# Hybrid encoder: feed-forward chunk 5 by seven products too, and other engines for some low parts and sums

## The chip, the core and the metric

The kernel runs on one NeuronCore of a Trainium2 chip. TensorE (PE in the profile) multiplies, VectorE (DVE) and ScalarE (ACT) work element by element, GpSimd (POOL) and SyncE (SP) mostly issue DMA transfers. The metric is device time in microseconds of one execution; the median of the timed runs counts.

## What is computed

Two layers over x, 512 tokens by 1024 channels, in float32: a gated linear attention, then a grouped-query attention, each followed by a gated feed-forward part with a convolution of width 3 over the tokens. The change acts in the feed-forward part alone:

```python
def conv_ffn(h, w_up, w_conv, b_conv, w_down):
    u = h @ w_up                              # 1024 -> 2 x 2816
    u = lax.conv_general_dilated(u, w_conv[:, None, :], window_strides=(1,),
        padding=[(1, 1)], dimension_numbers=('NWC', 'WIO', 'NWC'),
        feature_group_count=u.shape[-1]) + b_conv
    val, gate = jnp.split(u, 2, axis=-1)
    return (jax.nn.silu(gate) * val) @ w_down # 2816 -> 1024

x = x + conv_ffn(rmsnorm(x, norm_ffn[i]), ffn_w_up[i], ffn_w_conv[i], ffn_b_conv[i], ffn_w_down[i])
```

## The kernel before

Everything is held transposed: channels on the 128 partitions, the 512 tokens along the free axis. A float32 factor is used as a high part, rounded to fp32r by ScalarE, and a low part, the rest. Each product takes three matmuls: high by high, high by low, low by high.

The 2816 hidden channels are 22 **chunks** m of 128, each with a val half and a gate half. A *plain* chunk (`plain_up`) takes 2 halves x 8 input tiles x 3 = 48 matmuls of 128x512. A chunk *by seven* (`seven_up`, for the chunks in `SEVEN`) treats val and gate, two input tiles and the two halves of the tokens as a product of 2x2 blocks, done with seven products in place of eight: 7 products x 4 pairs of input tiles x 3 = 84 matmuls of 128x256. Its seven products (`go(1 ...)` to `go(7 ...)`, in the order 1, 6, 7, 4, 5, 2, 3) all issue at line 1099 in `product`. Product 1 of chunk m+1 is begun half-way through chunk m. Between products ScalarE copies partial sums from one PSUM bank to another (L1158 in `twice`, L1122, L1131), and VectorE adds one (L1161 in `add_seven`).

A chunk by seven needs four **weight pieces**. Piece 0 is two quarters as loaded; piece 1 and piece 2 come from sums: VectorE adds two quarters (L312, 1024 wide) or two DMA transfers do it into a tile `sum` (chunks in `SUMS_DMA`); L314 then makes piece 1's. Piece 3, half as wide, comes after L303. The high part is ScalarE's L341 (L305 for piece 3), the low part VectorE's L342 (L306); that is `split`. The other way is `low_dma`: ScalarE writes the high part (L291) and its negative (L292), and a transfer issued by POOL (L330) adds the weights onto the negative, which gives the low part. `UP_DMA` names the plain chunks whose low parts go that way, `LOW_0` the chunks whose piece 0 does. Weights are loaded by SP into five `raw` buffers and worked on in the order of the queue `W.todo`, up to six pieces ahead of use.

The products by seven also need sums of input tiles. `prepare_input(p)` makes them for pair p with four VectorE operations in the tile `xr` and `low_dma` into the tiles `xt`; `INPUT_AT` says after which chunk. Chunks 0 to 2 use the normal input, later ones the tiles `nh` and `nl`.

After val and gate come the convolution (ScalarE L1146, VectorE L1147 and L1148), SiLU (L1150) and the product of the two (L1151). Two chunks of results are a pair, which `prepare` turns into the inputs `gu` of the down-projection by seven: sums (L1174 to L1176, L1186), then high parts by ScalarE (L1167) and low parts by VectorE (L1168), or all by `low_dma` for the pairs in `Q_DMA`. The down-projection runs in two parts by seven, after chunks 9 and 17, four output groups each, and the rest plain at the end. `end` adds each output chunk to the residual and, in the last layer, stores it.

Each engine works through its own instructions in order. The order in which they stand is made by a scheduler from the code; `tc.high_priority` and `tc.issue_after` move some of them.

Of the kernel before, what the change touches and what calls it, by code (L numbers as in the profile page):

```python
# [8 lines left out]
F32 = mybir.dt.float32  # L9
# [51 lines left out]


NQ, NPART = 4, 2
PLAIN = ([(c, k) for c in range(4) for k in range(16, 20)] + [(c, k) for c in range(4) for k in (20, 21)]
         + [(c, k) for c in range(4, 8) for k in range(16, 22)])
# [12 lines left out]
SUMS_DMA = (12, 13, 14, 15, 16)  # L78
SUMS_NEAR = 6
LOW_0 = (7, 8)  # L80
LOW_1 = ()
LOW_2 = ()
STRIP_0 = ()
# [2 lines left out]
NH = 4  # L86
NL = 4
LOADS_FFN = 3
WIDE_AT = 1
BACK_AT = 20  # L90
PAW = 6
UPAW = 3
# [10 lines left out]
def hybrid_encoder_kernel(  # L103
# [71 lines left out]

    prm = cp.tile([P, PC_N], F32, name="prm")

    fold = lambda t: t.rearrange("p (o n) -> p o n", n=S)

    class Weights:  # L180

# [55 lines left out]
        def load(self, key):  # L237
            src, i, h = key
            if i < 0:
                self.load_vg(src, -i, h)  # L240
            elif (id(src), i) in self.sums:
                if (id(src), i) not in self.strip:
                    t1, t3 = (pair("raw", NR, F32, "raw") for _ in range(2))
                    sync.dma_start(fold(t1), self.outer(src, i))
                    e = self.totals.pop((id(src), i), None)
                    if e is None:
                        sync.dma_start(fold(t3), self.outer(src, i, 1))
                    else:
                        sync.dma_start(t3[:, S:], src[i, :, 3 * S :])
# [23 lines left out]
            self.made[id(src), i, h] = (hi, lo)  # L273

        def outer(self, src, i, first=0):
            return src[i].rearrange("p (q n) -> p q n", q=4)[:, first : first + 3 : 2, :]

        def total(self, src, i):
            if any(src is a and i in SUMS_DMA for a in up) and (id(src), i) not in self.totals:
                self.totals[id(src), i] = e = big(F32, "sum")  # L280
                sync.dma_start(e, src[i, :, : 2 * S])
                self.pending.append((e, src[i, :, S : 3 * S]))

        def two(self):
            self.turn += self.wide
# [9 lines left out]
        def summed(self, src, i, h):  # L295


            tiles = self.strip[id(src), i]
            r, t3, e = tiles if h == 0 else [tiles[h % 3]] + tiles[1:]
            if h == 3:  # L300
                del self.strip[id(src), i]
                r = t3[:, S:]
                dve.tensor_tensor(r, r, t3[:, :S], ALU.add)  # L303
                hi, lo = (sp.tile([P, S], F32R, tag="sq", bufs=3, name=nm(n)) for n in ("wh4", "wl4"))
                act.activation(hi, r, AF.Copy)  # L305
                self.last = dve.tensor_tensor(lo, r, hi.bitcast(F32), ALU.subtract)  # L306
                return hi, lo
            if h == 1:
                with tc.issue_after(self.last.ins) if self.last else ExitStack():
                    if e is None:  # L310
                        tiles[2] = e = pair("raw", NR, F32, "sum")
                        dve.tensor_tensor(fold(e), t3[:, :S].rearrange("p (o n) -> p o n", o=1).to_broadcast([P, 2, S]),  # L312
                                          fold(tiles[0]), ALU.add)
                    dve.tensor_tensor(t3[:, :S], e[:, S:], tiles[0][:, :S], ALU.add)  # L314
                tiles[0] = None
            hi, lo = self.two()
# [14 lines left out]
            self.pending = []  # L331

        def split(self, hi, lo, r, pieces=1, first=False):
            n = 2 * S // pieces
            for q in range(pieces):
                sl = slice(q * n, (q + 1) * n)
                a = r[q] if isinstance(r, list) else r[:, sl]
                if first and q == 0:
                    dve.tensor_copy(hi[:, sl], a)
                else:  # L340
                    act.activation(hi[:, sl], a, AF.Copy)  # L341
                dve.tensor_tensor(lo[:, sl], a, hi[:, sl].bitcast(F32), ALU.subtract)  # L342
# [32 lines left out]
    def add_ffn(layer):  # L375
        first = 0
        for m, part in DOWN_AFTER.items():
            add_up(layer, range(first, m + 1))
            W.add(down_w[layer], range(part * NQ, (part + 1) * NQ), 4)
            at = len(W.todo) - 4 * NQ - 1  # L380
            W.todo[at : at + 2] = W.todo[at + 1], W.todo[at]
            first = m + 1
        add_up(layer, range(first, FC))
        W.add(down_w[layer], range(NPART * NQ, down_w[layer].shape[0]))

    W.add(w_first)
    W.add(w_kq, range(MORE // 2))
# [654 lines left out]
    def ffn(layer, norm, cw, nxt):  # L1042
# [47 lines left out]
        def product(pieces, src, strip, pairs, i, dst, start):  # L1090
            h, o = PLACE[i]
            if h not in pieces:
                pieces[h] = W.piece(src, strip, h, PAW if W.wide else PA)
            wh, wl = pieces[h]
            for j, p in enumerate(pairs):
                sl = slice(o + j * P, o + (j + 1) * P)
                mh, ml = p[i]
                for a, (w, m) in enumerate(((wh, mh), (wh, ml), (wl, mh))):
                    mm(dst, w[:, sl], m, start=start and j == 0 and a == 0, stop=j == len(pairs) - 1 and a == 2,  # L1099
                       skip_group_check=True)  # L1100
            W.flush()

        def begin_up(m):
            if m in SEVEN:
                begun.append(seven_up(m))
                next(begun[-1])

        def seven_up(m):

# [24 lines left out]
            begin_up(m + 1)  # L1134
            go(2, r1, False)
            go(3, r2, False)
            yield 0, both
# [68 lines left out]
                           7: part(1), 6: part(3), 4: part(2)})  # L1206


        PLACE = {1: (0, 0), 4: (0, S), 6: (1, 0), 2: (1, S), 7: (2, 0), 5: (2, S), 3: (3, 0)}

        def down_part(part, m):

# [57 lines left out]
        for m in range(FC):  # L1270
            if m == BACK_AT:
                W.loads, W.wide = LOADS, 0
                x_load()
            elif m == WIDE_AT:
                W.loads, W.wide, W.turn = LOADS_FFN, 1, 1
            held.append(act_up(m))
            for p in INPUT_AT.get(m, ()):
                prepare_input(p)
# [2 lines left out]
                    pass  # L1281
            if m % 2 == 0:
                continue
            if m < 2 * NQ * NPART:
# [6 lines left out]
            held = []  # L1291
        cur, open_ = None, {}
        for u, (c, k) in enumerate(PLAIN):
            if u % 8 == 0:
# [243 lines left out]
def _layout(inputs):  # L1538
# [69 lines left out]
    order += [(k, n) for n, k in PLAIN]  # L1608
    k, n = np.array(order).T
    dn = dn.transpose(0, 1, 3, 2, 4)[:, k, n]  # L1610
    a["w_down"] = con(dn.reshape(2, -1, 16, P, P).transpose(0, 1, 3, 2, 4).reshape(2, -1, P, 4 * S))
    return a

# [18 lines left out]
```

## Time and profile before

| | |
|---|---|
| median of 3 timed runs | 1088.42 us (1088.01 to 1088.79) |
| the profiled execution's own time | 1090.41 us |
| its span | 1088.7 us |
| chunks 3 to 8 of layer 0 in the trace | 252 to 326 us |
| the same chunks in layer 1 | 775 to 844 us |
| TensorE busy | 1077.5 us in 6744 matmuls |
| loads and stores | 172.41 MB by DMA, 158 GB/s in the mean |

A profile row of the timeline has its start, its duration, the engine, the line, the operation with its tiles (buffer numbers left out) and, in brackets, how long the engine had been idle before it and what it was waiting for. A row of a table by stretches has the busy time of each engine in that stretch. TensorE's matmuls overlap in the pipeline, so the distance between starts is the cost of one, not its duration.

### The profile page before, as it was taken

How to read it: one execution, taken by the hardware profiler on the slowest of the kernel's cores; microseconds unless marked ns; L12 is line 12 of the kernel's file. 1: busy time of each engine (PE TensorE's matmuls, PEld its weight loads, DVE VectorE, ACT ScalarE, POOL GpSimd, SP SyncE). 2: the span in 40 equal slices, each digit the busy share in tenths (PEclk: the TensorE clock that was granted, in tenths of full speed). 3: DMA queues.
4: the chain of work that ended last, by engine and by line, in shares of the span. 5: the costliest groups of instructions: out<-in, count | busy, mean ns of one | idle time of the engine just before them, and what ended most of it. 6: DMA issues, size and time to landing. Idle time of an engine off the chain costs nothing.

```text
span 1088.7 us, 17624 instructions
## 1 busy us (share of the span) xinstructions
PE 1077.5 (99%) x6744; PEld 970.9 (89%) x6744; DVE 887.3 (82%) x1329; ACT 728.5 (67%) x1146; POOL 146.3 (13%) x163
## 2 busy tenths in 40 slices
PE   9999999999999999999999999999999999999998
PEld 8888988888899999999988888788889999999996
DVE  7998967569698899978855578765989989997882
ACT  8679575478676777667664677646976667865760
POOL 0212112021100200010014343002210020001000
PEclk9999999999899999999999999999999999999999
DMA  8744546599534882265757475558964388226552
GB/s 301 185 126 107 123 144 208 156 207 213 114 124 99 216 215 101 78 161 131 258 134 182 104 221 146 167 173 186 215 135 150 97 215 222 96 78 159 133 175 78
DMA packets 69141, 172.41 MB, mean 158 GB/s; under 512 B 6848, under 2 KB 7360, under 8 KB 69056
## 3 DMA queue, kind: packets, MB, share of 16 engines
q1 hardware_dynamic: 47616, 115.28, 32.2%
q0 software_dynamic: 16544, 47.46, 24.1%
q10 hardware_dynamic: 4896, 8.55, 2.1%
q8 instruction: 53, 0.87, 0.3%
q14 instruction: 32, 0.26, 0.1%
HBM read 122.76 MB, written 14.68 MB: 126 GB/s over the span
## 4 chain that ended last, share of the span: by engine, by line
PE 91%; DVE 3%; DMA 2%; ACT 2%; issue 1%; POOL 0%; SPq 0%; DVEq 0%; ACTq 0%; POOLq 0%
PE r L1099 39%; PE op L560 8%; PE vg L677 7%; PE up L507 5%; PE up L508 5%; PE up L509 5%; PE dn L508 2%; PE dn L507 2%; PE dn L509 2%; DMA raw<-in_w_up_dram 1%; PE av L534 1%; PE A L507 1%; PE A L509 1%; PE B L509 1%; PE B L507 1%
## 5 line engine op out<-in xcount | busy, mean ns | idle before, releaser
L342 DVE TENSOR_TENSOR wl<-raw,wh 128x1024 fp32r<-128x1024 f32 x156 | 189.6, 1218 | 28.0 <-ACT wh L341 27.6
L341 ACT ACTIVATE wh<-raw 128x1024 fp32r<-128x1024 f32 x156 | 161.8, 1052 | 68.6 <-PE op L560 20.7
L1099 PE MATMUL r<-xt,wh 128*128 128x256 f32 x896 | 163.9, 284 | 2.6 <-ACT r L1122 2.6
L1099 PE MATMUL r<-gu,wh 128*128 128x256 f32 x896 | 161.0, 282 | 0.0
L1099 PEld LDWEIGHTS r<-xt,wh 128*128 128x128 f32 x896 | 140.8, 193 | 3.0 <-ACT r L1122 2.8
L1099 PEld LDWEIGHTS r<-gu,wh 128*128 128x128 f32 x896 | 139.4, 190 | 0.7
L1099 PE MATMUL r<-xt,wl 128*128 128x256 f32 x448 | 127.7, 285 | 0.0
L1099 PE MATMUL r<-gu,wl 128*128 128x256 f32 x448 | 126.6, 283 | 0.0
L1099 PE MATMUL r<-nh,wh 128*128 128x256 f32 x336 | 96.5, 287 | 0.2 <-ACT r L1131 0.2
L1099 PE MATMUL r<-nh,wl 128*128 128x256 f32 x336 | 95.0, 283 | 0.0
L1099 PE MATMUL r<-nl,wh 128*128 128x256 f32 x336 | 95.0, 283 | 0.0
L1099 PEld LDWEIGHTS r<-xt,wl 128*128 128x128 f32 x448 | 86.4, 193 | 0.0
L1099 PEld LDWEIGHTS r<-gu,wl 128*128 128x128 f32 x448 | 85.2, 190 | 0.0
L560 PE MATMUL op<-oT,wh 128*128 128x512 f32 x256 | 72.4, 393 | 0.0
L1099 PEld LDWEIGHTS r<-nh,wh 128*128 128x128 f32 x336 | 64.2, 191 | 2.7 <-ACT r L1131 2.2
L291 ACT ACTIVATE wh<-raw 128x1024 fp32r<-128x1024 f32 x36 | 38.0, 1056 | 42.2 <-PE up L508 13.3
L1099 PEld LDWEIGHTS r<-nl,wh 128*128 128x128 f32 x336 | 64.3, 191 | 0.1
L1099 PEld LDWEIGHTS r<-nh,wl 128*128 128x128 f32 x336 | 64.2, 191 | 0.0
L508 PE MATMUL up<-nl,wh 128*128 128x512 f32 x160 | 62.7, 392 | 0.0
L507 PE MATMUL up<-nh,wh 128*128 128x512 f32 x160 | 62.7, 392 | 0.0
L509 PE MATMUL up<-nh,wl 128*128 128x512 f32 x160 | 62.7, 392 | 0.0
L342 DVE TENSOR_TENSOR wl<-sum,wh 128x1024 fp32r<-128x1024 f32 x44 | 53.7, 1219 | 5.6 <-ACT wh L341 5.4
(300 smaller groups left out, 2752.3 us busy)
## 6 DMA issues: line engine op xcount, KB each, us to landing
raw<-in_w_up_dram SPq DMA_DIRECT2D x74, 512.0 KB, 4.9
raw<-in_w_down_dram SPq DMA_DIRECT2D x44, 512.0 KB, 4.1
wl<-raw POOLq DMA_DIRECT2D x20, 512.0 KB, 5.0
wl<-in_w_up_dram POOLq DMA_DIRECT2D x16, 512.0 KB, 8.1
ring<-p ACTq DMA_DIRECT2D x32, 256.0 KB, 2.5
sum<-in_w_up_dram SPq DMA_DIRECT2D x10, 512.0 KB, 6.9
sum<-in_w_up_dram POOLq DMA_DIRECT2D x10, 512.0 KB, 7.0
raw<-in_w_up_dram SPq DMA_DIRECT2D x18, 256.0 KB, 4.0
```

What stands on the lines that cost most here:

```text
L291: act.activation(hi, r, AF.Copy)
L341: act.activation(hi[:, sl], a, AF.Copy)
L342: dve.tensor_tensor(lo[:, sl], a, hi[:, sl].bitcast(F32), ALU.subtract)
L507: mm(ps, wh, mh, start=start, stop=False)
L508: mm(ps, wh, ml, start=False, stop=False)
L509: return mm(ps, wl, mh, start=False, stop=stop)
L534: mm(ps[j][:, :width], hl[k][i == 2][:, j * P : (j + 1) * P], (wl if i == 1 else wh)[:, sl], start=k == 0 and i == 0, stop=k == KC - 1 and ...
L560: mm(pss[ng][n], wt[:, sl], mv, start=k == late[0][0] and i == 0, stop=k == late[-1][-1] and i == 2)
L677: last = mm(ps[j], m[:, js], w[:, sl], start=i in (1, 7, 2) and p == 0 and a == 0, stop=i in (4, 2, 3) and p == 3 and a == 2, skip_group_c ...
L1099: mm(dst, w[:, sl], m, start=start and j == 0 and a == 0, stop=j == len(pairs) - 1 and a == 2, skip_group_check=True)
```

## The change

- `SEVEN` gets chunk 5. In `W.todo` the exchange of two entries where chunks by seven begin moves from chunk 6 to chunk 5.
- `INPUT_AT`: pair 3's input is prepared after chunk 3 with pair 2's, not after chunk 4.
- `UP_DMA`: of the plain chunks, 1, 2 and 4 get their low parts by DMA; before it was 1, 2 and 5.
- `LOW_0` is empty: piece 0 of chunks 7 and 8 is split by ScalarE and VectorE.
- `SUMS_DMA`: chunks 12 and 13 get their sums on VectorE, 14 to 16 by DMA as before.
- `Q_DMA`: pair 6's low parts are made by `low_dma`.
- `end`: the last output chunk is added in one operation and stored by one transfer; before it went in two halves over two queues.

All but the last hold for both layers. The remaining code of the diff (`TAIL`, `TAILED`, `tail_part`, `view`, `begin`) stands for a third way of the down-projection's rest; with `TAILED = ()` and `TAIL = 100` none of it runs. The layout of the weights in memory follows `SEVEN`. Its core:

```diff
-SEVEN = (6, 7, 8, 10, 11, 12, 13, 14, 15, 16, 18, 19, 20, 21)
+SEVEN = (5, 6, 7, 8, 10, 11, 12, 13, 14, 15, 16, 18, 19, 20, 21)
...
-INPUT_AT = {2: (0, 1), 3: (2,), 4: (3,)}
-Q_DMA = ()
-UP_DMA = (1, 2, 5)
-SUMS_DMA = (12, 13, 14, 15, 16)
+INPUT_AT = {2: (0, 1), 3: (2, 3)}
+Q_DMA = (6,)
+UP_DMA = (1, 2, 4)
+SUMS_DMA = (14, 15, 16)
 SUMS_NEAR = 6
-LOW_0 = (7, 8)
+LOW_0 = ()
...
-                if t == 0 and m not in DOWN_AFTER:
-                    begin_up(m + 1)
-                if t == 0 and m in DOWN_AFTER:
-                    down.append(down_part(DOWN_AFTER[m], m))
-                    next(down[-1])
+                if t == 0:
+                    begin(m)
...
-        def end(c, ps):
-            if nxt is not None or c < KC - 1:
+        def end(c, ps, last=False):
+            if nxt is not None or not last:
                 dve.tensor_tensor(x[c], x[c], ps, ALU.add)
```

The changed kernel is longer, so its lines have other numbers: L291 and L292 become L304 and L305, L303 and L306 L316 and L319, L312 and L314 L325 and L327, L330 L343, L341 and L342 L354 and L355, L1099 L1119, L1122 L1152, L1131 L1161, L1147 and L1148 L1177 and L1178, L1151 L1181, L1158 L1188.

ScalarE in layer 0's chunk 6, before. `r_2771` is the tile of chunk 6's partial sums, `raw_2679` the loaded quarters of chunk 8's piece 0:

```order
L341 ACTIVATE wh_2675<-raw_2631 128x1024
L1146 ACTIVATE y_2727<-up_2698,cw 128x512
L291 ACTIVATE wh_2774<-raw_2679 128x1024
L1122 ACTIVATE r_2771<-r_2696 128x256
L292 ACTIVATE wl_2775<-raw_2679 128x1024
L1158 ACTIVATE u_2791<-r_2773 128x512
L305 ACTIVATE wh_2755<-raw_2631 128x512
L1150 ACTIVATE y_2727<-y_2727 128x512
```

The same place in the changed kernel; here `r_2826` is chunk 6's, and `raw_2607` and `raw_2608` hold chunk 7's quarters:

```order
L1188 ACTIVATE r_2756<-r_2732 128x512
L318 ACTIVATE wh_2665<-raw_2559 128x512
L1176 ACTIVATE y_2728<-u_2700,cw 128x512
L1152 ACTIVATE r_2826<-r_2756 128x256
L1176 ACTIVATE y_2786<-r_2623,cw 128x512
L1188 ACTIVATE u_2845<-r_2828 128x512
L354 ACTIVATE wh_2770<-sum_2733 128x1024
L354 ACTIVATE wh_2736<-raw_2608 128x1024
```

The copy of chunk 6's partial sums (L1122, now L1152) stood right behind the high part of chunk 8's piece 0 (L291); now it stands between convolution starts, and the high parts that follow belong to chunk 7.

VectorE at chunk 8's pieces in layer 0, before; `raw_2679` and `raw_2680` are its quarters, `wl_2828` is piece 1's low part, `wl_2860` piece 2's:

```order
L312 TENSOR_TENSOR sum_2824<-raw_2680,raw_2679 128x1024
L1147 SCALAR_TENSOR_TENSOR y_2879<-r_2696,cw,y_2879 128x511
L314 TENSOR_TENSOR raw_2680<-sum_2824,raw_2679 128x512
L1148 SCALAR_TENSOR_TENSOR y_2879<-r_2696,cw,y_2879 128x511
L1151 TENSOR_TENSOR y_2879<-y_2879,y_2819 128x512
L342 TENSOR_TENSOR wl_2828<-raw_2680,wh_2827 128x1024
L342 TENSOR_TENSOR wl_2860<-sum_2824,wh_2859 128x1024
L303 TENSOR_TENSOR raw_2680<-raw_2680 128x512
```

And in the changed kernel, where `raw_2740` and `raw_2741` are chunk 8's quarters, `wl_2882` is piece 1's low part and `wl_2914` piece 2's:

```order
L325 TENSOR_TENSOR sum_2878<-raw_2741,raw_2740 128x1024
L1177 SCALAR_TENSOR_TENSOR y_2873<-u_2845,cw,y_2873 128x511
L327 TENSOR_TENSOR raw_2741<-sum_2878,raw_2740 128x512
L1178 SCALAR_TENSOR_TENSOR y_2873<-u_2845,cw,y_2873 128x511
L355 TENSOR_TENSOR wl_2914<-sum_2878,wh_2913 128x1024
L1177 SCALAR_TENSOR_TENSOR y_2933<-r_2756,cw,y_2933 128x511
L355 TENSOR_TENSOR wl_2882<-raw_2741,wh_2881 128x1024
L1178 SCALAR_TENSOR_TENSOR y_2933<-r_2756,cw,y_2933 128x511
L316 TENSOR_TENSOR raw_2741<-raw_2741 128x512
L1181 TENSOR_TENSOR y_2933<-y_2933,y_2873 128x512
```

Piece 2's low part now comes first, and both stand ahead of the addition L1181, which ends the convolution.

GpSimd's transfers from chunk 4 on in layer 0, before:

```order
L330 DMA wl_2481<-in_w_up_dram 128x1024
L330 DMA xt_2435<-xr_2212 128x1024
L330 DMA wl_2575<-in_w_up_dram 128x1024
L330 DMA xt_2443<-xr_2219 128x1024
L330 DMA xt_2524<-xr_2226 128x1024
L330 DMA xt_2618<-xr_2233 128x1024
L330 DMA wl_2669<-in_w_up_dram 128x2x512
L330 DMA wl_2775<-in_w_up_dram 128x2x512
```

And in the changed kernel:

```order
L343 DMA wl_2387<-in_w_up_dram 128x1024
L343 DMA xt_2434<-xr_2212 128x1024
L343 DMA wl_2478<-in_w_up_dram 128x1024
L343 DMA xt_2442<-xr_2219 128x1024
L343 DMA xt_2521<-xr_2226 128x1024
L343 DMA xt_2529<-xr_2233 128x1024
```

Chunk 4's low parts (`wl`, 128x1024) take the place of chunk 5's, pair 3's `xt` follows pair 2's at once, and the two transfers for chunks 7 and 8 (128x2x512) are gone.

More of the change, by code (lines that the diff above doesn't have):

```diff
@@ L88 @@
 LOADS_FFN = 3
+TAIL_SUMS = ()
 WIDE_AT = 1
+TURN = 1
 BACK_AT = 20
@@ L242, in load @@
                 if (id(src), i) not in self.strip:
-                    t1, t3 = (pair("raw", NR, F32, "raw") for _ in range(2))
+                    v, n = self.view(src, i)
+                    t1, t3 = (pair("raw", NR, F32, "raw")[:, : 2 * n] for _ in range(2))
                     sync.dma_start(fold(t1), self.outer(src, i))
@@ L275, in outer, with view @@
         def outer(self, src, i, first=0):
-            return src[i].rearrange("p (q n) -> p q n", q=4)[:, first : first + 3 : 2, :]
-        def total(self, src, i):
[L279 to L282, printed above, removed]
+            return self.view(src, i)[0].rearrange("p (q n) -> p q n", q=4)[:, first : first + 3 : 2, :]
+        def view(self, src, i):
+            if i < TAIL:
+                return src[i], S
+            row, part = divmod(i - TAIL, 2)
+            return src[NPART * NQ + row, :, part * 2 * S : (part + 1) * 2 * S], S // 2
+        def total(self, src, i):
+            if i in (SUMS_DMA if any(src is a for a in up) else TAIL_SUMS) and (id(src), i) not in self.totals:
+                v, n = self.view(src, i)
+                self.totals[id(src), i] = e = big(F32, "sum")[:, : 2 * n]
+                sync.dma_start(e, v[:, : 2 * n])
+                self.pending.append((e, v[:, n : 3 * n]))
         def two(self):
@@ L380, in add_ffn @@
             at = len(W.todo) - 4 * NQ - 1
-            W.todo[at : at + 2] = W.todo[at + 1], W.todo[at]
+            if m not in SEVEN:
+                W.todo[at : at + 2] = W.todo[at + 1], W.todo[at]
             first = m + 1
         add_up(layer, range(first, FC))
-        W.add(down_w[layer], range(NPART * NQ, down_w[layer].shape[0]))
+        if layer not in TAILED:
+            W.add(down_w[layer], range(NPART * NQ, down_w[layer].shape[0]))
+            return
+        w = down_w[layer]
+        for n in range(NQ):
+            W.sums.add((id(w), TAIL + n))
+            W.todo += [(w, TAIL + n, h) for h in range(4)]
+            if n % 2:
+                W.todo.append((w, NPART * NQ + NTAIL, n // 2))
     W.add(w_first)
@@ L1106, in begin_up, with begin @@
                 next(begun[-1])
+            if m == FC and layer in TAILED:
+                begun.append(tail_part())
+                next(begun[-1])
+        def begin(m):
+            if m in DOWN_AFTER:
+                down.append(down_part(DOWN_AFTER[m], m))
+                next(down[-1])
+            else:
+                begin_up(m + 1)
         def seven_up(m):
@@ L1254, in down_part, with tail_part, first, rest @@
                 W.pending.append((c, g))
-        def end(c, ps):
-            if nxt is not None or c < KC - 1:
+        def tail_part():
+            pairs = [quads.pop(NPART * NQ + i) for i in range(NTAIL)]
+            pieces = [{} for _ in range(NQ)]
+            go = lambda n, *a: product(pieces[n], w_dn, TAIL + n, pairs, *a)
+            st = {}
+            def first(n):
+                r = bank("pt", "r1")[:, :H]
+                go(n, 1, r, True)
+                st[n] = bank("acc", "r")
+                with tc.high_priority(200):
+                    twice(st[n], r)
+            def rest(n, cur):
+                for o, (c, ps) in enumerate(((2 * n + 1, third[n]), (2 * n, st[n]))):
+                    for k in range(2):
+                        at = ((n % 2) * 4 + 2 * o + k) * P
+                        sl = slice(at, at + P)
+                        mh, ml = plain[FC - 2 + k]
+                        for a, (w, mv) in enumerate(((cur[0], mh), (cur[0], ml), (cur[1], mh))):
+                            mm(ps, w[:, sl], mv, start=False, stop=k == 1 and a == 2, skip_group_check=True)
+                    end(c, ps, n == NQ - 1 and o == 1)
+            third = {}
+            first(0)
+            yield
+            for n in range(NQ):
+                r1, r2 = st[n][:, :H], st[n][:, H:]
+                go(n, 6, r2, False)
+                third[n] = r3 = bank("s", "r3")
+                with tc.high_priority(200):
+                    act.activation(r3[:, :H], r2, AF.Copy, scale=-1.0)
+                r4 = bank("pt", "r4")[:, :H]
+                go(n, 7, r4, True)
+                f = tmp("u", "f")
+                with tc.high_priority(200):
+                    twice(f, r4)
+                go(n, 4, r3[:, :H], False)
+                dve.tensor_tensor(x[2 * n + 1], x[2 * n + 1], f, ALU.add)
+                go(n, 5, r2, False)
+                with tc.high_priority(200):
+                    act.activation(r3[:, H:], r2, AF.Copy, scale=-1.0)
+                if n % 2 == 0:
+                    first(n + 1)
+                go(n, 2, r1, False)
+                go(n, 3, r2, False)
+                if n % 2:
+                    cur = W.half(w_dn, 2 * (NPART * NQ + NTAIL) + n // 2)
+                    rest(n - 1, cur)
+                    if n + 1 < NQ:
+                        first(n + 1)
+                    rest(n, cur)
@@ L1291, in ffn @@
             held = []
+        for steps in begun:
+            for _ in steps:
+                pass
+            return
         cur, open_ = None, {}
```

44 lines of the change are left out of this document (26 added, 18 removed).

## The prediction

> **What bounds the kernel now.** I read the page first, for the busy shares, then the chain that ended last, then TensorE's waits, and last the stretches of both layers' chunks 3 to 8, where the change acts.
>
> ```profile
> PE 1077.5 (99%) x6744; PEld 970.9 (89%) x6744; DVE 887.3 (82%) x1329; ACT 728.5 (67%) x1146; POOL 146.3 (13%) x163
> PEclk9999999999899999999999999999999999999999
> PE 91%; DVE 3%; DMA 2%; ACT 2%; issue 1%; POOL 0%; SPq 0%; DVEq 0%; ACTq 0%; POOLq 0%
> ```
>
> TensorE is the bound: 99% busy and 91% of the chain. Only two things can shorten such a kernel: fewer or cheaper matmuls, and the few places where TensorE waits or is clocked down. One of the forty clock digits is an 8, at about 272 to 299 us. TensorE's waits, the longest first, name one line with such a wait:
>
> ```profile
> PE r L1099 <- ACT r L1122: 2.6, 1, 2.6
> PE warm L423 <- DVE bd L429: 1.3, 1, 1.3
> ```
>
> The columns are the total, the count and the longest. L1099 is a product of a chunk by seven, L1122 ScalarE's copy between two products of a half. Both layers run the same code over chunk 3 up to the first piece of the down-projection's first part, so I set the two stretches side by side (columns: length, TensorE busy, granted clock, DMA share, GB/s):
>
> ```profile
> 251.95:326.65 74.70, 72.11 (x423) 0.95 0.58 140
> 775.31:844.50 69.19, 69.19 (x424) 1.00 0.61 152
> ```
>
> Layer 0 takes 74.70 - 69.19 = **5.51 us** longer: 74.70 - 72.11 = 2.59 is idle, and the other 2.92 is work at a lower clock. The timeline shows where:
>
> ```profile
> 290.72 1.06 ACT L291 ACTIVATE wh<-raw 128x1024 fp32r<-128x1024 f32 x1 [3.11 <-DMA raw<-in_w_up_dram]
> 291.69 0.37 ACT L1122 ACTIVATE r<-r 128x256 f32<-128x256 f32 x1
> 292.10 0.80 PE L1099 MATMUL r<-xt,wh 128*128 128x256 f32 x2 [2.59 <-ACT r L1122]
> 292.91 0.63 PE L1099 MATMUL r<-xt,wh 128*128 128x256 f32 x2
> 293.55 0.63 PE L1099 MATMUL r<-xt,wh 128*128 128x256 f32 x2
> ```
>
> ScalarE takes its work in order. L291, the high copy of chunk 8's first weight piece, waits 3.11 us for that piece's load; L1122, whose product has ended by then, stands behind it, and TensorE behind L1122. The load itself is a piece of the chain, issued at 281.50 (start, us):
>
> ```profile
> 281.50 9.20 DMA raw<-in_w_up_dram
> ```
>
> Afterwards three matmuls take 0.64 us (292.91 to 293.55), 0.213 each, until about 298. Full rate is this row of the chain in layer 1 (start, us, matmuls):
>
> ```profile
> 810.01 25.80 PE r L1099 x216
> ```
>
> 25.80 / 216 = 0.1194 us per 128x256 matmul.
>
> **The change, part by part.** *Chunk 5 by seven.* A plain chunk is 48 matmuls of 128x512. In layer 1, where nothing waits, chunk 3 starts at the first row here and chunk 4 at the second:
>
> ```profile
> 775.31 0.40 PE L507 MATMUL up<-nh,wh 128*128 128x512 f32 x1
> 786.35 0.39 PE L507 MATMUL up<-nh,wh 128*128 128x512 f32 x1
> ```
>
> That is 11.04 us. By seven it is 84 x 0.1194 = 10.03: 1.01 us less. The longest run of such matmuls gives a little less:
>
> ```profile
> 851.33 106.61 PE r L1099 x888
> ```
>
> 106.61 / 888 = 0.1201, 10.08 a chunk, 0.96 less. I take 0.98 in each layer: **-1.96 us**.
>
> *LOW_0 empty.* Chunks 7 and 8's first pieces no longer go through L291, L292 and a DMA; they are split by ScalarE (high) and VectorE (low). In the new order the copy between products (now L1152) comes right after work whose inputs are there: ahead of it in chunk 6 stand a copy of r, the high part of a piece 3 and a convolution start, no copy of a weight just loaded. So the 2.59 us wait goes, and with it the slow stretch: **-5.51 us** in layer 0, nothing in layer 1, which has neither.
>
> *VectorE's new work.* This pays for both. Its groups between 230 and 350 us (the mean ns of one stands behind the comma):
>
> ```profile
> L342 DVE TENSOR_TENSOR wl<-raw,wh 128x1024 fp32r<-128x1024 f32 x17 | 20.7, 1217 | 1.4 <-ACT wh L341 1.4
> L312 DVE TENSOR_TENSOR sum<-raw,raw 128x1024 f32<-128x1024 f32 x6 | 7.3, 1217 | 0.0
> L303 DVE TENSOR_TENSOR raw<-raw 128x512 f32<-128x512 f32 x6 | 4.1, 682 | 0.0
> L306 DVE TENSOR_TENSOR wl<-raw,wh 128x512 fp32r<-128x512 f32 x5 | 3.5, 690 | 0.4 <-PE r L1099 0.3
> ```
>
> Chunk 5 adds one sum and three low parts of 1024 columns (4 x 1.217), and four operations of 512 (4 x 0.69: L314, L303, L306 and the addition L1161): 7.63 us. Successive starts are some 0.08 closer than the durations (below, 308.33 is followed by an operation at 309.47 in the same view), so 7.63 - 8 x 0.08 = 7.0. UP_DMA takes two low parts off (chunk 4; chunk 5's had no VectorE work before), LOW_0 puts two on: net **+7.0 us** of VectorE work up to chunk 8 in each layer, while TensorE comes to it 0.98 us earlier, and in layer 0 5.51 more. Can VectorE hold that? Its idle time (columns: PE, PEld, DVE, ACT, POOL busy, clock, DMA share, GB/s):
>
> ```profile
> 270.00:280.00 10.00, 10.00 (x47) 8.26 (x47) 7.72 (x13) 7.53 (x11) 0.86 (x1) 1.00 0.37 71
> 280.00:290.00 10.00, 9.51 (x57) 8.25 (x56) 8.83 (x12) 4.47 (x7) 1.10 (x1) 1.00 0.87 189
> 290.00:300.00 10.00, 7.90 (x43) 7.90 (x44) 4.34 (x8) 6.34 (x11) 1.10 (x1) 0.66 0.49 109
> 300.00:310.00 10.00, 10.00 (x86) 10.00 (x86) 9.32 (x14) 7.25 (x14) 0.00 (x0) 1.00 0.31 105
> 792.00:802.00 10.00, 10.00 (x45) 8.15 (x44) 7.90 (x16) 7.14 (x11) 1.59 (x2) 1.00 0.43 83
> 802.00:812.00 10.00, 10.00 (x60) 8.79 (x58) 8.57 (x11) 6.84 (x10) 1.23 (x2) 1.00 0.81 163
> 812.00:822.00 10.00, 10.00 (x86) 10.00 (x85) 8.72 (x17) 8.14 (x15) 1.10 (x1) 1.00 0.58 153
> 822.00:832.00 10.00, 10.00 (x86) 10.00 (x86) 9.90 (x14) 6.97 (x12) 0.00 (x0) 1.00 0.47 160
> ```
>
> The tightest piece is chunk 8's second. Its low part, and TensorE's first use, in layer 0 and layer 1:
>
> ```profile
> 308.33 1.22 DVE L342 TENSOR_TENSOR wl<-raw,wh 128x1024 fp32r<-128x1024 f32 x1
> 312.37 0.28 PE L1099 MATMUL r<-xt,wl 128*128 128x256 f32 x1
> 826.46 1.22 DVE L342 TENSOR_TENSOR wl<-raw,wh 128x1024 fp32r<-128x1024 f32 x1
> 830.16 0.28 PE L1099 MATMUL r<-xt,wl 128*128 128x256 f32 x1
> ```
>
> The margins are 312.37 - 309.55 = 2.82 and 830.16 - 827.68 = 2.48 us. Layer 1: VectorE idles 2.10 + 1.43 + 1.28 = 4.81 us ahead of it (792 to 822); if the new work fills all of that, the piece is 7.0 - 4.81 = 2.2 later and needed 0.98 earlier: 2.48 - 2.2 - 0.98 = -0.7. Layer 0: idle is 2.28 + 1.17 + 5.66 + 0.68 = 9.79, so the piece can be 2.8 earlier, but is needed 5.51 + 0.98 earlier: 2.82 + 2.8 - 6.49 = -0.9. The new order gives some of that back. Before, VectorE made this low part after the chunk's sum, two convolution steps each of val and gate, L314 and the addition L1151; now the low part of the sum comes first and this one second, both ahead of that addition, and TensorE takes the sum's product between the first matmuls of the other. So the first of the two low parts stands one operation of 0.6 us earlier, and the second is needed some six matmuls (0.7 us) later. That leaves -0.1 and -0.3. The bounds: no wait at all, or, if none of layer 1's idle time is filled, 7.0 + 0.98 - 2.48 = 5.5 us. I take 0.3 in each layer, near to the balance of the rows: **+0.6 us**.
>
> *The rest.* Pair 3's input is prepared a chunk earlier, and has to be, since chunk 5 reads it. Its low part arrives by a transfer. Here are the median times to landing (between 225 and 330 us) and, in layer 0, the issue of pair 2's:
>
> ```profile
> xt<-xr POOLq DMA_DIRECT2D x4, 512.0 KB, 5.0
> raw<-in_w_up_dram SPq DMA_DIRECT2D x11, 512.0 KB, 5.8
> ```
>
> ```profile
> 268.75 0.86 POOL L330 DMA_DIRECT2D xt<-xr  x1 [4.71 <-DVE xr L1198]
> ```
>
> Pair 3's now follows at once, at about 269.6, and lands at 274.6; as late by the median as the load above (9.20 against 5.8), at 278. Chunk 5 needs it last of the pairs: 251.95 + 2 x 11.04 + 1.43 (its first product, 12 matmuls) + 9 x 0.1194 = 276.5. I cost it at nothing; up to 1.5 us if a slow transfer falls there. SUMS_DMA adds two sums (2 x 1.14 of VectorE's time) at chunks 12 and 13, and Q_DMA takes low parts of three 512 columns and one 256 (3 x 0.61 + 0.3) off after chunk 13: net +0.15 over some 30 us of TensorE's work, so nothing; should the sums come late once, a wait of at most their 2.3 us. Two sum transfers fewer on SP and four new ones of pair 6 on POOL lie beside TensorE's work: pair 6 is first read in the second down part, after three and a half chunks, 35 us. The last output chunk is added and stored whole:
>
> ```profile
> 1084.89 0.75 DVE L1265 TENSOR_TENSOR x<-x,dn 128x256 f32<-128x256 f32 x2 [3.39 <-PE dn L509]
> 1085.34 0.33 SPq L1266 DMA_DIRECT2D out_dram<-x  x1
> 1085.67 0.36 ACTq L1266 DMA_DIRECT2D out_dram<-x  x1
> ```
>
> Two halves end 0.75 us after the start, and the second transfer is issued at 1085.67. One addition of 512 takes 0.69, its issue follows at about 1085.6, and the transfer is twice as large: **+0.15** (between 0 and 0.3).
>
> *The sum.* The profiled execution took 1090.41, 1.71 more than its span and 1.99 more than the median of 1088.42. 1090.41 - 5.51 - 1.96 + 0.6 + 0.15 = 1083.7. If the 1.99 is the same for both kernels, the median after is 1081.7; if it lies in the stall (a load that came sooner in the timed runs), 1083.7. Nothing in the trace tells these apart; I take the middle, **1082.7 us**, -0.5%.
>
> **A rule weighed.** Here a wait of 2.59 us was followed by a clock of 0.66 in 290 to 300 and cost 5.51 in all. The Trainium skill, "TensorE: Matmul & The Clock Gate", section "Why this matters for your kernels", says that only idle gaps above about 3 us bring the clock down. The row disagrees: 2.59 was enough. By the rule, a new wait below 3 us would cost its length alone, and two of 2.6 would leave about 1087 instead of 1093.
>
> **Rivals.** *1. The wait moves* (1087.9, chance 0.18). VectorE is late in one layer by about 2.6 us and the clock falls again: 1082.7 - 0.3 + 5.5 = 1087.9. For it: the balances of -0.7 and -0.9 before reordering. Against: VectorE ran 9.9 of 10 at 822 to 832, so it does fill up when work is queued. The change then brings nothing that could be told from no change.
>
> *2. VectorE becomes the bound, in both layers* (1093, chance 0.12): slower. By 822 to 832 it is full (9.90 of 10) even while the first pieces of chunks 7 and 8 go by DMA; these two low parts (2 x 1.14) and chunk 5's pieces come on top, so the debt builds from chunk 5 on. It decides from a wait of 2.6 us in each layer, that is when about 1.9 of layer 1's 4.81 us of idle time stay idle behind loads; price 2 x 5.5: 1082.7 - 0.6 + 11.0 = 1093.1. Against: chunk 5's pieces are work that VectorE can take up in just that idle time, since their loads now stand ahead of chunk 6's on SP.
>
> *3. The wait was the profile's alone* (1087.2, chance 0.04). If the load had landed 2 us sooner in the timed runs than the 9.20 us of the profiled one, a wait of 0.6 us would be left, and the median had nothing to lose but chunk 5: 1088.42 - 1.96 + 0.75 = 1087.2. Against: then the profiled execution should be 4 to 5 us above the median, and it is 1.99.
>
> **How the numbers follow.** Forecast 0.66, rivals 0.18, 0.12 and 0.04. Faster by over 0.2% (below 1086.24; 0.2% is about what a measurement of this kernel can tell from no change) is the forecast: 0.66. Within 0.2% are rivals 1 and 3: 0.22. Slower is rival 2: 0.12. The range goes from 1080.5 (the constant in whole and no new wait: 1081.7 - 0.6 = 1081.1, and 0.6 below it for the smaller terms) to 1088.0, rival 1's upper end; the forecast's own range is 1080.5 to 1085.
>
> **What would show it.** Right: no TensorE wait on the copy L1152 in chunk 6, a clock of 1.00 from 280 to 300, and both layers' stretches from chunk 3 to the down part at 68.2 us plus at most a few tenths. VectorE above 9.5 in 270 to 310. Rival 1 or 2: a wait of TensorE's products for VectorE's low part wl, in chunks 5 to 8. Wrong would be a chunk 5 that isn't near 10.03 us, or a wait for a transfer (xt, raw) at 275 to 283.

## The result and the profile after

| | before | changed |
|---|---|---|
| median, us (6 runs each) | 1088.09 (1083.88 to 1088.79) | 1082.29 (1081.75 to 1082.90) |
| profiled execution's own time, us | 1090.41 | 1081.80 |
| its span, us | 1088.7 | 1080.1 |

The ratio is 0.9946, with a 95% interval of 0.9930 to 0.9963: 0.5% faster, against a forecast of 1082.7. The kernel before varies by 5 us from run to run, the changed one by 1.2.

The page of the changed kernel: busy times, the granted clock by slices, the chain.

```profile
PE 1072.3 (99%) x6816; PEld 970.3 (90%) x6816; DVE 898.8 (83%) x1340; ACT 734.5 (68%) x1162; POOL 145.5 (13%) x163
PEclk9999999999999999999999999999999999999999
PE 94%; DVE 2%; ACT 1%; DMA 1%; issue 1%; POOL 0%; SPq 0%; ACTq 0%; POOLq 0%; DVEq 0%
```

The one 8 in the row of the clock has gone, and TensorE's share of the chain rose from 91% to 94%. TensorE's waits, the longest first (total, count, longest):

```profile
PE warm L445 <- DVE bd L451: 1.3, 1, 1.3
PE kv L529 <- ACT ga L791: 0.6, 1, 0.6
```

No product of a chunk by seven (L1119) is among them any more. The two layers' stretches from chunk 3 up to the first piece of the down-projection's first part (length, TensorE busy, clock, DMA share, GB/s):

```profile
251.92:319.83 67.91, 67.91 (x460) 1.00 0.52 135
767.71:835.67 67.96, 67.96 (x460) 1.00 0.52 135
```

Both layers take the same time now: 74.70 became 67.91 in layer 0 (-6.79), 69.19 became 67.96 in layer 1 (-1.23). VectorE, third busy column after TensorE and its weight loads, is full there:

```profile
290.00:300.00 10.00, 10.00 (x86) 10.00 (x85) 10.00 (x17) 6.82 (x13) 0.00 (x0) 1.00 0.16 58
300.00:310.00 10.00, 10.00 (x83) 9.81 (x82) 10.00 (x14) 8.69 (x13) 0.00 (x0) 1.00 0.48 155
```

And the tight piece, the low part of chunk 8's piece 1: VectorE's row, and TensorE's first use of it in layer 0.

```profile
305.24 1.21 DVE L355 TENSOR_TENSOR wl<-raw,wh 128x1024 fp32r<-128x1024 f32 x1
```

```profile
306.36 0.28 PE L1119 MATMUL r<-xt,wh 128*128 128x256 f32 x1
306.51 0.38 PE L1119 MATMUL r<-xt,wl 128*128 128x256 f32 x1
306.73 0.40 PE L1119 MATMUL r<-xt,wh 128*128 128x256 f32 x2
```

The low part ends at 306.45, and TensorE reads it at 306.51. The distances 0.15 and 0.22 in place of 0.12 show that the chain of matmuls was held up by about 0.1 us. Layer 1 looks the same (ready at 821.43, read at 821.49). So VectorE's margin of 2.8 and 2.5 us is used up to the last tenth, and no more than that.

### The profile page after: what moved, and what is told of

It reads as the page before. It is cut to its first block, busy times and chain, and to the rows that moved or that the text cites. A ratio compares the mean times of both kernels' runs of the same rounds, so it can differ in the third digit from the quotient of the medians.

```text
span 1080.1 us, 17776 instructions
## 1 busy us (share of the span) xinstructions
PE 1072.3 (99%) x6816; PEld 970.3 (90%) x6816; DVE 898.8 (83%) x1340; ACT 734.5 (68%) x1162; POOL 145.5 (13%) x163
## 4 chain that ended last, share of the span: by engine, by line
PE 94%; DVE 2%; ACT 1%; DMA 1%; issue 1%; POOL 0%; SPq 0%; ACTq 0%; POOLq 0%; DVEq 0%
PE r L1119 43%; PE op L582 8%; PE vg L699 7%; PE up L529 5%; PE up L531 5%; PE up L530 5%; PE dn L530 2%; PE dn L529 2%; PE dn L531 2%; PE av L556 1%; PE A L529 1%; PE A L531 1%; PE B L529 1%; PE B L531 1%; PE A L530 1%; PE B L530 1%
## 5 line engine op out<-in xcount | busy, mean ns | idle before, releaser
L355 DVE TENSOR_TENSOR wl<-raw,wh 128x1024 fp32r<-128x1024 f32 x160 | 194.3, 1217 | 33.0 <-ACT wh L354 32.7
L354 ACT ACTIVATE wh<-raw 128x1024 fp32r<-128x1024 f32 x160 | 167.3, 1052 | 67.1 <-PE op L582 20.7
L1119 PE MATMUL r<-xt,wh 128*128 128x256 f32 x960 | 173.3, 282 | 0.0
L1119 PE MATMUL r<-gu,wh 128*128 128x256 f32 x896 | 162.0, 282 | 0.0
L1119 PEld LDWEIGHTS r<-xt,wh 128*128 128x128 f32 x960 | 148.9, 190 | 0.3
L1119 PEld LDWEIGHTS r<-gu,wh 128*128 128x128 f32 x896 | 139.7, 190 | 1.2 <-ACT r L1274 0.2
L1119 PE MATMUL r<-xt,wl 128*128 128x256 f32 x480 | 135.9, 283 | 0.0
L1119 PE MATMUL r<-gu,wl 128*128 128x256 f32 x448 | 126.6, 283 | 0.0
L1119 PE MATMUL r<-nh,wh 128*128 128x256 f32 x360 | 102.2, 284 | 0.0
L1119 PE MATMUL r<-nh,wl 128*128 128x256 f32 x360 | 101.8, 283 | 0.0
L1119 PE MATMUL r<-nl,wh 128*128 128x256 f32 x360 | 101.5, 282 | 0.0
L1119 PEld LDWEIGHTS r<-xt,wl 128*128 128x128 f32 x480 | 91.2, 190 | 0.2
L1119 PEld LDWEIGHTS r<-gu,wl 128*128 128x128 f32 x448 | 85.2, 190 | 0.2
L1119 PEld LDWEIGHTS r<-nh,wh 128*128 128x128 f32 x360 | 68.5, 190 | 1.8 <-ACT r L1161 1.6
L1119 PEld LDWEIGHTS r<-nl,wh 128*128 128x128 f32 x360 | 68.5, 190 | 0.1
L1119 PEld LDWEIGHTS r<-nh,wl 128*128 128x128 f32 x360 | 68.6, 190 | 0.0
L304 ACT ACTIVATE wh<-raw 128x1024 fp32r<-128x1024 f32 x32 | 33.8, 1056 | 37.4 <-PE up L530 11.5
L355 DVE TENSOR_TENSOR wl<-sum,wh 128x1024 fp32r<-128x1024 f32 x46 | 56.0, 1217 | 3.9 <-ACT wh L354 3.9
L582 PEld LDWEIGHTS op<-oT,wh 128*128 128x128 f32 x256 | 47.4, 188 | 9.7 <-ACT oT L984 0.3
L354 ACT ACTIVATE wh<-sum 128x1024 fp32r<-128x1024 f32 x46 | 48.3, 1050 | 7.0 <-DVE sum L325 6.8
L529 PE MATMUL up<-nh,wh 128*128 128x512 f32 x128 | 50.2, 392 | 0.0
```

The costliest lines, as they stand in the source:

```text
L529: mm(ps, wh, mh, start=start, stop=False)
L582: mm(pss[ng][n], wt[:, sl], mv, start=k == late[0][0] and i == 0, stop=k == late[-1][-1] and i == 2)
```

## The experiments

Three theories stood for the wait of 2.59 us in chunk 6 of layer 0. **A**, as predicted: it belongs to the way of chunk 8's piece 0 by L291 and a transfer, which LOW_0 switches. **B**: the place of the copy on ScalarE counts, and only chunk 5 by seven moves it. **C**: the load is late because GpSimd's transfer for chunk 7 runs beside it. In each run below, the ratio is to runs of the kernel before on the same chip.

### 1. LOW_0 empty, nothing else

```diff
-LOW_0 = (7, 8)
+LOW_0 = ()
```

> The kernel before with LOW_0 empty and nothing else changed. In the new order a high part of chunk 8's piece 0 still stands right ahead of the copy L1122 on ScalarE (L341 in place of L291), behind the same load. Theory A, as predicted (the wait belongs to the way by L291 and its transfer): the wait and the slow clock are gone, 5.5 us less than 1088.1, about 1082.6 with chunk 5 still plain. Theory B (the place of the copy is what counts, and only chunk 5 by seven moves it): the wait of 2 to 3 us on L1122 stays, 1088 within 0.7. Theory C (GpSimd's transfer of chunk 7's low part, issued 0.24 us before the load of chunk 8's piece 0, slows that load to 9.2 us): with it gone the load lands in about 6 us, no wait, 1082.6 to 1083.9.

Measured: 1084.89 against 1088.29, ratio 0.9972 (0.9960 to 0.9984). ScalarE at the place (timeline of this run):

```profile
286.78 0.76 ACT L1146 ACTIVATE y<-up,cw 128x512 f32<-128x512 f32 x1
287.44 1.05 ACT L341 ACTIVATE wh<-raw 128x1024 fp32r<-128x1024 f32 x1
288.39 0.37 ACT L1122 ACTIVATE r<-r 128x256 f32<-128x256 f32 x1
```

The wait is gone, though the high part of chunk 8's piece 0 (now L341) still stands right ahead of L1122: it doesn't wait, since the load had landed. That excludes B as the only cause. The time is 1.0 to 2.3 us above what A and C gave. From one profiled execution to the other 5.60 us went (1090.41 to 1084.81), between the medians 3.40: the wait was worth less in the timed runs than in the profiled one.

### 2. and 3. One of the two chunks at a time

```diff
-LOW_0 = (7, 8)
+LOW_0 = (7,)
```

> The kernel before with LOW_0 = (7,): chunk 7's low part still comes by a transfer, chunk 8's piece 0 no longer goes by L291. Theory A: no wait, about 1082.6. Theories B and C: the wait stays, 1088 within 0.7, since the copy stands where it stood and chunk 7's transfer is still there beside the load.

```diff
-LOW_0 = (7, 8)
+LOW_0 = (8,)
```

> The kernel before with LOW_0 = (8,): chunk 8's piece 0 still goes by L291 right ahead of L1122, but chunk 7's transfer by GpSimd is gone. Theories A and B: the wait stays, 1088 within 0.7. Theory C: the load lands in about 6 us, the wait is gone, 1082.6 to 1083.9.

Measured: LOW_0 = (7,) 1089.13 (1084.77 to 1091.33), ratio 1.0006 (0.9992 to 1.0019); LOW_0 = (8,) 1084.87, ratio 0.9968 (0.9956 to 0.9980), 1.0 above C's range. With (7,), chunk 8's piece no longer goes by L291, and yet ScalarE waits for its load and TensorE for ScalarE (timeline):

```profile
289.30 1.06 ACT L341 ACTIVATE wh<-raw 128x1024 fp32r<-128x1024 f32 x1 [1.73 <-DMA raw<-in_w_up_dram]
290.27 0.37 ACT L1122 ACTIVATE r<-r 128x256 f32<-128x256 f32 x1
290.57 0.58 ACT L1158 ACTIVATE u<-r 128x512 f32<-128x512 f32 x1
```

```profile
290.69 0.50 PE L1099 MATMUL r<-xt,wh 128*128 128x256 f32 x2 [1.22 <-ACT r L1122]
```

This execution took 1085.93 us, less than eight of the ten runs; how long the wait was in the others isn't recorded.

With (8,) L291 stands where it stood, and nothing waits:

```profile
287.37 1.05 ACT L291 ACTIVATE wh<-raw 128x1024 fp32r<-128x1024 f32 x1
288.32 0.37 ACT L1122 ACTIVATE r<-r 128x256 f32<-128x256 f32 x1
```

The transfers issued from 281 to 292 us, first with (7,), then with (8,) (median us from issue to landing behind the size):

```profile
raw<-in_w_up_dram SPq DMA_DIRECT2D x2, 512.0 KB, 7.9
wl<-in_w_up_dram POOLq DMA_DIRECT2D x1, 512.0 KB, 9.3
```

```profile
raw<-in_w_up_dram SPq DMA_DIRECT2D x2, 512.0 KB, 4.7
wl<-in_w_up_dram POOLq DMA_DIRECT2D x1, 512.0 KB, 6.0
```

The two loads are the same, and the first of them is issued at the same time (281.45 and 281.35). In the first case chunk 7's transfer runs beside them, in the second only chunk 8's, which starts at 289.96, when they have landed. Theory C holds, A falls: the transfer of chunk 7, not the way of chunk 8's piece, makes the load late.

### 4. Chunk 5 plain again in the changed kernel

```diff
-SEVEN = (5, 6, 7, 8, 10, 11, 12, 13, 14, 15, 16, 18, 19, 20, 21)
+SEVEN = (6, 7, 8, 10, 11, 12, 13, 14, 15, 16, 18, 19, 20, 21)
```

> The changed kernel with chunk 5 plain again (SEVEN without 5; everything else as changed). Chunk 8's copy stands ahead of the copy of partial sums again, as in the kernel before, but no transfer of chunk 7's low part runs. Theories A and C: no long wait, so only chunk 5's matmuls come back: 1082.3 + 2 x 1.25 = 1084.8. Theory B: the wait comes back as well, 1088 to 1090.

Measured: 1083.91 (1082.72 to 1085.12), ratio 0.9961 (0.9947 to 0.9975); no wait in chunk 6, only one of 0.43 us on the copy L1152 at 310.54, and the clock at 1.00. A and C gave 1084.8, B at least 1088, so the place of the copy alone doesn't bring the wait back. Its interval overlaps that of the changed kernel, so the timed runs alone don't give the worth of chunk 5; the stretches above do.

### 5. Two low parts more on VectorE

```diff
-UP_DMA = (1, 2, 4)
+UP_DMA = (1, 2)
```

> The changed kernel with UP_DMA = (1, 2): chunk 4's two low parts go to VectorE (2 x 1.14 = 2.3 us more of its work ahead of chunk 8), and nothing else. In the changed kernel the low part of chunk 8's piece 1 is ready 0.06 us (layer 0) and 0.05 us (layer 1) before TensorE begins to use it, and VectorE is busy 10.0 of 10 us from 290 to 310. Theory V (VectorE is at its limit there, the slack is nil): a wait of TensorE for wl of about 2 us in each layer; 1082.3 + 4.5 = 1086.8 if the clock holds, up to 1093 if it falls as it did after the 2.59 us wait. Rival (the order adapts, since the work is interleaved differently and other places have slack of 2 to 5 us): under 1 us in all, 1082.3 to 1083.3.

Measured: 1091.30 (1089.00 to 1096.70), ratio 1.0029 (1.0012 to 1.0045): slower than the kernel before. TensorE's waits:

```profile
PE r L1119 <- DMA xt<-xr: 5.3, 2, 2.9
PE r L1119 <- ACT r L1161: 1.2, 1, 1.2
```

L1161 is the copy that was L1131. The time lies in theory V's range, but the wait shows at another place than expected: VectorE comes later to the inputs of pair 3, their transfer is issued at 272.49, in the changed kernel at 268.55, and chunk 5 waits for it. The transfer itself also took longer, 7.2 us to landing, where the four such transfers of the changed kernel took 4.5 to 5.5. This is the price of the prediction's second rival, though by an input's transfer and not by a low part of VectorE: run 7, on the same chip and as fast as the changed kernel, had 1082.56, which is 8.7 us less.

### 6. and 9. The later chunks as before

```diff
-Q_DMA = (6,)
-SUMS_DMA = (14, 15, 16)
+Q_DMA = ()
+SUMS_DMA = (12, 13, 14, 15, 16)
...
-            if nxt is not None or not last:
+            if nxt is not None or c < KC - 1:
```

> The changed kernel with SUMS_DMA = (12, 13, 14, 15, 16), Q_DMA empty and the last output chunk in two halves over two queues, as before the change. By the prediction these three were worth +0.15 in all: 1082.1, the same as the changed kernel within 0.4. Rival: part of the gain that the predicted terms leave open comes from them, then 1082.7 to 1084.

Measured: 1084.54 (1083.99 to 1085.86), ratio 0.9958 (0.9944 to 0.9973); run 7, on the same chip, had 1082.56. The rival holds, at 0.5 us above its range. TensorE at chunk 16 of layer 0:

```profile
427.48 0.40 PE L1119 MATMUL r<-xt,wh 128*128 128x256 f32 x2
428.08 0.51 PE L1119 MATMUL r<-xt,wh 128*128 128x256 f32 x2 [0.21 <-ACT wh L354]
428.89 0.39 PE L1119 MATMUL r<-xt,wl 128*128 128x256 f32 x1 [0.30 <-DVE wl L355]
```

Four matmuls (two rows of two) take the 1.41 us from 427.48 to 428.89, where four pitches of 0.12 make 0.48: 0.93 lost, and as much in layer 1. Which of the three edits is it?

```diff
-SUMS_DMA = (14, 15, 16)
+SUMS_DMA = (12, 13, 14, 15, 16)
```

> The changed kernel with SUMS_DMA = (12, 13, 14, 15, 16) alone put back; Q_DMA and the end stay as changed. In the run with all three put back TensorE waited about 1 us at chunk 16 in each layer, for a high part and a low part, 0.2 to 0.3 at a time. If pair 6's low parts on VectorE made that wait (they come right ahead of chunk 16's pieces, whose margin in the changed kernel is 0.1 us): this one has no such wait, 1082.3 within 0.4. If the sums' transfers made it: 1083.5 to 1084.5, with the wait at chunk 16.

Measured: 1083.05 (1082.20 to 1085.56), ratio 0.9950 (0.9935 to 0.9965), and no wait of a product by seven. The median lies between the two expected ranges; the trace decides, and it isn't the sums alone. The end in two halves can't make a wait at chunk 16, and took the same time: from the last matmul's start to the end of the span 1083.2 - 1078.94 = 4.26 us in two halves, 1080.1 - 1075.86 = 4.24 whole. Pair 6's low parts on VectorE remain, by elimination: no run changes Q_DMA alone.

### 7. LOW_0 as before in the changed kernel

```diff
-LOW_0 = ()
+LOW_0 = (7, 8)
```

> The changed kernel with LOW_0 = (7, 8) again. VectorE has 2.3 us less to do ahead of chunk 8; chunk 7's transfer by GpSimd runs beside the loads of chunk 8's quarters again, and chunk 8's high part stands ahead of the copy L1161 of chunk 6. Theory C (that transfer makes the load late): the load lands 8 to 9 us after its issue at about 283, so at about 292, where ScalarE comes to it at about 291: a wait of 0.5 to 1 us at most in layer 0, 1082.3 to 1083.3, so the emptied LOW_0 matters little once chunk 5 is by seven. Theory A (the way by L291 is what costs): the wait of 2.6 us and the lower clock come back, 1086 to 1088.

Measured: 1082.56 (1081.83 to 1083.90), ratio 0.9940 (0.9925 to 0.9955): the same as the changed kernel. ScalarE in chunk 6 of layer 0:

```profile
287.69 0.37 ACT L1152 ACTIVATE r<-r 128x256 f32<-128x256 f32 x1 [0.72 <-PE r L1119]
291.44 1.05 ACT L304 ACTIVATE wh<-raw 128x1024 fp32r<-128x1024 f32 x1
292.39 0.37 ACT L1161 ACTIVATE r<-r 128x256 f32<-128x256 f32 x1
```

The copy L1152 waits for TensorE alone; the high part of chunk 8's piece 0 comes 3.8 us later, ahead of the next copy, and finds its load landed. That load was issued at 283.66, and although chunk 7's transfer followed it at 284.00, it landed after 5.6 us, not the 8 to 9 that theory C expected. So that transfer doesn't always make the load late; what decides it, whether the order of issue (here the load went first) or the other loads beside it, is not shown. With chunk 5 by seven the emptied LOW_0 is not needed: either of the two takes the wait away.

### 8., 10. and 11. More chunks by seven

Chunk 4, with the sums of chunks 5 to 8 and a low part of chunk 8 by DMA to relieve VectorE:

```diff
-SEVEN = (5, 6, 7, 8, 10, 11, 12, 13, 14, 15, 16, 18, 19, 20, 21)
+SEVEN = (4, 5, 6, 7, 8, 10, 11, 12, 13, 14, 15, 16, 18, 19, 20, 21)
...
-INPUT_AT = {2: (0, 1), 3: (2, 3)}
+INPUT_AT = {2: (0, 1, 2, 3)}
...
-UP_DMA = (1, 2, 4)
-SUMS_DMA = (14, 15, 16)
+UP_DMA = (1, 2, 3)
+SUMS_DMA = (5, 6, 7, 8, 14, 15, 16)
...
-LOW_0 = ()
+LOW_0 = (8,)
```

> Chunk 4 by seven as well: SEVEN with 4, INPUT_AT = {2: (0, 1, 2, 3)}, UP_DMA = (1, 2, 3), the sums of chunks 5 to 8 by DMA, LOW_0 = (8,). TensorE's work falls by 1.25 us in each layer. VectorE's ahead of chunk 8 changes by +7.0 (chunk 4) - 2.3 (chunk 3's low parts) - 4.6 (four sums) - 1.1 (one low part) = -1.0, against 1.25 of TensorE's time less. If VectorE's total is what counts: 1080 to 1081. If the sums' transfers, which are twice as many bytes beside the loads, make loads late, or all four pairs' inputs after chunk 2 come late for chunk 4: 1083 to 1090.

Measured: 1104.57, ratio 1.0136 (1.0121 to 1.0151). TensorE waits for four inputs `xt` and two low parts `wl`, both transfers:

```profile
PE r L1119 <- DMA xt<-xr: 11.2, 4, 5.6
PE up L531 <- DMA wl<-in_w_up_dram: 4.9, 2, 3.0
```

Chunk 17, and then chunk 9, each from the changed kernel:

```diff
-SEVEN = (5, 6, 7, 8, 10, 11, 12, 13, 14, 15, 16, 18, 19, 20, 21)
+SEVEN = (5, 6, 7, 8, 10, 11, 12, 13, 14, 15, 16, 17, 18, 19, 20, 21)
...
-SUMS_DMA = (14, 15, 16)
+SUMS_DMA = (14, 15, 16, 17)
...
-LOW_0 = ()
+LOW_0 = (16, 17)
```

> The changed kernel with chunk 17 by seven too: SEVEN with 17, its sum by DMA (SUMS_DMA = (14, 15, 16, 17)), piece 0 of chunks 16 and 17 by DMA (LOW_0 = (16, 17)). TensorE has 1.0 to 1.3 us less to do in each layer. VectorE: +7.0 for chunk 17, -2.3 for its two plain low parts, -1.1 for its sum, -2.3 for two low parts by DMA: +1.3, and 1.25 less time. The margin after chunk 17 is 7.1 us in the changed kernel, so that holds if chunk 16's 0.1 us of margin does (two low parts of 1.1 are taken off just there): 1079.8 to 1080.5. If VectorE's limit is met at chunk 17's own pieces: waits of up to 2 us a layer, 1081 to 1084.

```diff
-SEVEN = (5, 6, 7, 8, 10, 11, 12, 13, 14, 15, 16, 18, 19, 20, 21)
+SEVEN = (5, 6, 7, 8, 9, 10, 11, 12, 13, 14, 15, 16, 18, 19, 20, 21)
...
-SUMS_DMA = (14, 15, 16)
+SUMS_DMA = (9, 14, 15, 16)
...
-LOW_0 = ()
+LOW_0 = (8, 9)
```

> The changed kernel with chunk 9 by seven too: SEVEN with 9, its sum by DMA (SUMS_DMA = (9, 14, 15, 16)), piece 0 of chunks 8 and 9 by DMA (LOW_0 = (8, 9)). By the same sum as for chunk 17: TensorE 1.0 to 1.3 us less in each layer, VectorE +1.3 behind chunk 8, where the margin is 8 us, and 1.1 less ahead of chunk 8's piece 1, where it is nil: 1079.8 to 1080.5. If chunk 9's piece 0, needed half-way through chunk 8, comes while VectorE is still full with chunk 8's (10.0 of 10 us): waits of 1 to 3 us a layer, 1082 to 1088.

Measured: 1092.52, ratio 1.0046 (1.0029 to 1.0062), and 1090.20, ratio 1.0018 (1.0002 to 1.0033). The longest wait in the run with chunk 17, then in the run with chunk 9:

```profile
PE r L1119 <- DMA wl<-in_w_up_dram: 5.9, 2, 3.4
```

```profile
PE r L1119 <- DMA wl<-in_w_up_dram: 4.0, 2, 3.1
```

Relief by DMA put a transfer on the path: the piece 0 that goes by `low_dma` comes later than TensorE wants it. All three runs came out above every range that was expected of them: the expectations counted mainly VectorE's work, and the longest waits were for transfers. None of the three beats the changed kernel.

### 12. Chunk 5 alone

The changed kernel with the three other settings as before:

```diff
-Q_DMA = (6,)
+Q_DMA = ()
...
-SUMS_DMA = (14, 15, 16)
+SUMS_DMA = (12, 13, 14, 15, 16)
...
-LOW_0 = ()
+LOW_0 = (7, 8)
```

> The kernel before with chunk 5 by seven and what it needs (INPUT_AT, UP_DMA) and the end in one piece, and nothing else: LOW_0 = (7, 8), SUMS_DMA = (12, 13, 14, 15, 16) and Q_DMA empty stay as before. If chunk 5's new order takes the copy L1161's neighbours out of the load's way by itself, and pair 6's low parts on VectorE are what holds chunk 16 up: no wait in chunks 5 to 8 (as with LOW_0 alone put back), waits of 0.5 to 1 us in each layer at chunk 16, 1083.5 to 1084.5. If the two low parts fewer on VectorE at chunks 7 and 8 let it catch up by chunk 16: no wait there either, 1082.3 within 0.5. If the wait of chunk 6 comes back: 1086 to 1088.

Measured: 1084.81 (1084.33 to 1085.02), ratio 0.9959 (0.9945 to 0.9972). Nothing waits in chunks 5 to 8; TensorE's waits at chunk 16 of the two layers are those of run 6:

```profile
PE r L1119 <- DVE wl L355: 0.6, 2, 0.3
PE r L1119 <- ACT wh L354: 0.4, 2, 0.2
```

The first outcome holds, at 0.3 us above its range. Run 7 differs from this one in pair 6's transfer and the sums, and the sums alone made no wait in run 9; so the difference is about what pair 6's transfer is worth: 1082.56 against 1084.81 by the medians (of two chips), 0.9940 against 0.9959 by the ratios.

## Why the prediction was right, point by point

- **The stall and its clock, -5.51.** It went, as predicted, and with it the slow clock. The size is right for the profiled execution (layer 0's stretch lost 6.79, layer 1's 1.23: 5.56 between them). In the timed runs the wait was smaller: runs 1 and 3, without it, are worth 1088.29 - 1084.87 = 3.4. So the 1.99 us between the profiled execution and the median did lie in the stall for the most part; the changed kernel's profiled execution, which has no stall, is 0.5 below its median. That is the reading by which the prediction would have come to 1083.7. Its middle of 1082.7 was nearer to the measured 1082.29 by luck: the rest of the change gave 1.9 us more than the sum had ("The sum", below).
- **Why it went.** Here a step was wrong: "Chunks 7 and 8's first pieces no longer go through L291, L292 and a DMA", with the wait put down to the place of L291 alone. Runs 1 to 3 show that L291 may stand there; what made the load take 9.2 us was chunk 7's transfer, issued 0.24 us ahead of it. The order did change as the prediction read it, but by run 1 that comes from chunk 5 by seven, not from LOW_0, and by run 7 it is enough without the emptied LOW_0. So two causes of the gain overlap, and taking LOW_0 back costs nothing.
- **Chunk 5, -0.98 a layer.** Measured -1.23 in layer 1, whose stretch had no wait to lose. 1.01 of it is the better row's figure. The plain matmuls beside it started 0.2288 us apart in the mean, before 0.2307, which is 0.23 over 120 of them; why isn't traced.
- **New waits, +0.6.** About 0.1 in each layer. The bounds reached up to 5.5; the balance of VectorE's work (-0.1 and -0.3 us) was near the truth: the low part is ready 0.06 us before it is read. Run 5 shows that 2.3 us more of such work makes the kernel slower than before (ratio 1.0029), so a time like the second rival's was near, by another path: one entry of UP_DMA away.
- **Pair 6 and the sums, nothing.** The step "net +0.15 over some 30 us of TensorE's work, so nothing" failed. The kernel before has no wait at chunk 16, and chunk 5 by seven brings one there (run 12): without pair 6's transfer TensorE loses 0.93 us a layer. Where the work lies counted, not its net: the sums come before, pair 6's low parts right ahead of chunk 16's pieces. How chunk 5 uses up the margin so far behind is not shown; VectorE isn't simply late all the way, for in run 12 it works only 7.31 of the 10 us from 350 to 360.
- **The end, +0.15.** Measured nothing (4.24 us before and after, from the last matmul's start to the end).
- **The sum.** From one profiled execution to the other, 8.61 us: 6.79 and 1.23 in the two stretches, 0.51 between the first stretch and layer 1's attention (251.56 to 251.05), 0.1 elsewhere. The forecast had 6.7 (1090.41 to 1083.7): 1.9 less, of which 1.15 is chunk 5 with its new waits, 0.15 the end, and the rest lies outside the terms of the sum.
- **The rule on the clock.** The trace spoke against the 3 us of the Trainium skill ("TensorE: Matmul & The Clock Gate", "Why this matters for your kernels"), and so do further waits: one of 2.48 us brought the clock down too (last section).

## What to carry to other kernels

Before a wait behind a load is put down to the order of the instructions, look at what else was on the DMA queues when the load was issued: a transfer that nobody waits for yet can be the cause. When work is moved to an engine that fills up, the cost can show far behind the change, as at chunk 16 here: look at the tight pieces beyond it too. And a profiled execution that is slower than the median by a good part of a stall suggests that the stall varies from run to run.

## What the runs showed of the hardware

Two loads of 512 KB, issued 2 us apart, landed after 4.7 to 4.8 us in the median by themselves (runs 3 and 1) and after 7.9 us with a third transfer of 512 KB issued 0.23 us ahead on another queue (run 2). With such a transfer issued 0.34 us behind it, a load landed after 5.6 us (run 7). TensorE's granted clock stayed at 1.00 after waits of 1.22 us (run 2) and 2.33 us (run 5, layer 0), and fell after 2.48 us (run 10, layer 0: 0.50 from 1 to 4 us behind it), 2.59 us (before) and 2.94 us (run 5, layer 1). After the last one the matmuls started 0.21 us apart, as they did in the kernel before; the rows are of run 5:

```profile
800.75 0.53 PE L1119 MATMUL r<-xt,wh 128*128 128x256 f32 x1 [2.94 <-DMA xt<-xr]
801.08 0.42 PE L1119 MATMUL r<-xt,wl 128*128 128x256 f32 x1
801.29 0.41 PE L1119 MATMUL r<-xt,wh 128*128 128x256 f32 x1
801.51 0.41 PE L1119 MATMUL r<-xt,wl 128*128 128x256 f32 x1
```
